# Splitting the end of the first layer's two MLPs into halves of 256 tokens

## The chip, the cores and the metric

The kernel runs on one core of a Trainium2 chip. The metric is the device time of one execution in microseconds (us): the median of several executions. Its work is spread over five engines, each of which works through its own list of instructions in order: TensorE (PE: matmuls), VectorE (DVE), ScalarE (ACT), GpSimd (POOL) and SyncE (SP), which mostly starts transfers. Waits between engines are semaphores.

## What is computed

A trunk of two layers over 1,024 tokens of width 1,024. Each layer is a token mixer and a squared-ReLU MLP with 4,096 hidden columns, with a norm before and after each and a residual around each. The mixer of layer 1 is a diagonal state-space model (S5), that of layer 2 an attention in which an indexer picks the keys.

```python
for i in range(DEPTH):                       # 2 layers
    pre = rms_norm(h, norm_g[i, 0])
    mix = s5_mixer(pre, ...) if i % 2 == 0 else dsa_mixer(pre, ...)
    h = h + rms_norm(mix, norm_g[i, 1])
    ff = sq_relu_mlp(rms_norm(h, norm_g[i, 2]), mlp_w1[i], mlp_w2[i])
    h = h + rms_norm(ff, norm_g[i, 3])

def sq_relu_mlp(h, w1, w2):
    a = jax.nn.relu(h @ w1)
    return (a * a) @ w2
```

## The kernel before

**Layout.** Tokens are worked in two halves of 512 (half 0 and half 1). An activation is held feature-major: four blocks `[128, 2, 512]`, so that 1,024 features are 4 blocks by 2 by 128 partitions, and the 512 tokens run along the row. Every fp32 operand of a large matmul is split into a rounded part `hi` and a rest `lo`, and each product is three matmuls (`mm3`, L157 to L159). Of a weight unit (`unit`) ScalarE writes `hi` (L140), and `lo` is written by VectorE for the unit's first part and by GpSimd for its second (both L141).

**An MLP** (`mlp`) makes hidden pairs (w1) and, a chunk of them later, adds their products with w2: eight chunks c, in each four blocks d by two rows j, of 12 matmuls into one PSUM tile `m`. VectorE adds each tile to the block `acc` in SBUF (L334). The path `finish` (L310 to L320) was there already: chunk 7 loads its four w2 units first and then runs twice over them, tokens 0 to 255 and then 256 to 511, with matmuls of 256 columns and an add of 256 columns (L319), and calls `finish` after each. Before the change only the very last MLP of the program uses it.

**The end of an MLP.** `post_norm` squares the outputs on ScalarE, sums the blocks on VectorE (`squares`, L191), sums over partitions with a matmul by a column of ones (L194), takes the reciprocal root (`rsqrt`, L165 to L169), spreads it over the partitions with transposes (L236), copies that to `rb` (ScalarE, L238), scales (VectorE, L250) and adds the residual (L260: blocks 0 and 2 on VectorE, 1 and 3 on GpSimd), which is loaded into tiles `ld` from `hd`. Then `pre_norm` makes the next inputs: `hi` on ScalarE (L206), `lo` on VectorE (L207), squares, their sums (L191) and the sum over partitions (L194), and from it r (L212 to L216). `att_r` multiplies rope's table by r (L1144 on VectorE, L1151 on ScalarE) and transposes it (L1153 on TensorE); the index and query projections of layer 2 follow.

**The order on each engine.** A scheduler lays the instructions out from a simulated timeline of its own; code under `high_priority` is put forward. Beside each MLP runs other work ("side"), a step after so many of the MLP's units, and where the side work or an end waits, the matmuls of the following MLP stand between as filler. So the end of half 0's MLP in layer 1 is laid among the first w1 matmuls of half 1's MLP; the end of half 1's among the attention outputs (`att_in`) of half 0 and the next MLP's w1 matmuls. The body of `run` sets the sequence:

```python
acc = self.mlp(0, xn[1][0], first(), PER_A, WAIT_A)
xo = finished(self.att_in(0, "x"))
x1, r = self.pre_norm(residual(1, acc, 3, hd[0], hd[1], xn[1][1]), 4, square=False)
self.att_r(1, r)
```

Below, "the first end" is that of half 0's MLP of layer 1, "the second end" that of half 1's.

## Time and profile before

| | |
|---|---|
| time, median of 3 runs | 2282.32 us (2281.85 to 2283.55) |
| the profiled execution | 2287.54 us, its span 2285.6 us |
| mean granted TensorE clock | 0.971 of full speed |
| TensorE busy with matmuls | 2166.6 us, 95% |
| VectorE, ScalarE, GpSimd busy | 63%, 47%, 31% |

Everything below is read from one profiled execution, whose own time is 1.94 us over its span (from the first instruction to the last). It is 5.2 us over the median of the runs. A wait stands in brackets behind the instruction that ended it, with the engine and line that released it. "PEclk" is the clock granted to TensorE, as a share of full speed.

### The profile page before, as it was taken

How to read it: one execution, taken by the hardware profiler on the slowest of the kernel's cores; microseconds unless marked ns; L12 is line 12 of the kernel's file. 1: busy time of each engine (PE TensorE's matmuls, PEld its weight loads, DVE VectorE, ACT ScalarE, POOL GpSimd, SP SyncE). 2: the span in 40 equal slices, each digit the busy share in tenths (PEclk: the TensorE clock that was granted, in tenths of full speed). 3: DMA queues.
4: the chain of work that ended last, by engine and by line, in shares of the span. 5: the costliest groups of instructions: out<-in, count | busy, mean ns of one | idle time of the engine just before them, and what ended most of it. 6: DMA issues, size and time to landing. Idle time of an engine off the chain costs nothing.

```text
span 2285.6 us, 29529 instructions
## 1 busy us (share of the span) xinstructions
PE 2166.6 (95%) x10376; PEld 1785.5 (78%) x10376; DVE 1436.7 (63%) x2775; ACT 1083.0 (47%) x2027; POOL 701.8 (31%) x588
## 2 busy tenths in 40 slices
PE   6999999999989999999988988999999899999996
PEld 3577778888878888888877766888788687888886
DVE  9566953333656598555677898989767467332335
ACT  4434643333353475555363455677457354423332
POOL 2004542222336522221346533221210035222223
PEclk9999999999999999999989999999999999999998
DMA  7002533333337653445346543433332444433231
GB/s 276 27 30 83 181 123 94 100 95 100 111 114 204 165 134 107 119 101 167 132 159 157 154 119 81 110 86 92 88 84 60 134 131 164 138 95 99 93 105 51
DMA packets 115893, 266.81 MB, mean 117 GB/s; under 512 B 14241, under 2 KB 49569, under 8 KB 115745
## 3 DMA queue, kind: packets, MB, share of 16 engines
q1 hardware_dynamic: 101984, 240.80, 33.9%
q0 software_dynamic: 12672, 23.07, 5.3%
q8 instruction: 82, 1.34, 0.3%
q10 hardware_dynamic: 1088, 1.05, 0.1%
q14 instruction: 67, 0.54, 0.1%
HBM read 229.02 MB, written 34.67 MB: 115 GB/s over the span
## 4 chain that ended last, share of the span: by engine, by line
PE 73%; DVE 15%; ACT 6%; issue 4%; DMA 1%; POOL 1%; SPq 0%; ACTq 0%; DVEq 0%; POOLq 0%
PE m L158 18%; PE m L157 18%; PE m L159 18%; PE p L1036 2%; PE p L1056 2%; PE p L157 2%; PE p L159 2%; PE p L158 2%; DVE wh L141 2%; PE p L1064 1%; DVE b L250 1%; PE p L1065 1%; ACT junk L974 1%; DVE b L207 1%; PE m L611 1%
## 5 line engine op out<-in xcount | busy, mean ns | idle before, releaser
L157 PE MATMUL m<-b,wh 128*128 128x512 f32 (+1 forms) x2208 | 860.5, 392 | 26.1 <-DVE acc L334 9.7
L158 PE MATMUL m<-b,wh 128*128 128x512 f32 (+1 forms) x2208 | 858.0, 391 | 4.6 <-DVE b L207 4.0
L159 PE MATMUL m<-b,wh 128*128 128x512 f32 (+1 forms) x2208 | 856.3, 390 | 4.3 <-DVE wh L141 4.3
L141 POOL TENSOR_TENSOR wh<-wr,wh 128x512 fp32r<-128x512 f32 (+1 forms) x346 | 448.7, 1302 | 1281.6 <-ACT wh L140 1261.6
L140 ACT ACTIVATE wh<-wr 128x512 fp32r<-128x512 f32 (+1 forms) x692 | 400.0, 592 | 503.2 <-PE m L159 413.9
L157 PEld LDWEIGHTS m<-b,wh 128*128 128x128 f32 x2208 | 419.4, 190 | 115.8 <-DVE acc L334 10.8
L159 PEld LDWEIGHTS m<-b,wh 128*128 128x128 f32 x2208 | 418.9, 190 | 88.8 <-DVE wh L141 5.1
L158 PEld LDWEIGHTS m<-b,wh 128*128 128x128 f32 x2208 | 419.2, 190 | 87.3 <-DVE b L207 4.8
L141 DVE TENSOR_TENSOR wh<-wr,wh 128x512 fp32r<-128x512 f32 (+1 forms) x346 | 273.4, 797 | 296.8 <-ACT wh L140 283.2
L334 DVE TENSOR_TENSOR acc<-acc,m 128x512 f32<-128x512 f32 x216 | 147.1, 682 | 155.5 <-PE m L159 153.5
L299 ACT ACTIVATE b<-m 128x512 f32<-128x512 f32 x128 | 76.2, 595 | 179.0 <-PE m L159 175.8
L148 DVE CAST b<-b 128x1024 fp32r<-128x1024 f32 x68 | 59.9, 881 | 135.5 <-ACT b L301 126.4
L159 PE MATMUL p<-b,wh 128*128 128x512 f32 (+1 forms) x304 | 116.1, 391 | 8.4 <-DVE wh L141 8.4
L157 PE MATMUL p<-b,wh 128*128 128x512 f32 (+1 forms) x304 | 115.8, 398 | 5.7 <-ACT b L721 3.4
L158 PE MATMUL p<-b,wh 128*128 128x512 f32 (+1 forms) x304 | 117.3, 391 | 0.0
L1043 ACT ACTIVATE s<-s,ring 128x128 f32<-128x128 f32 (+7 forms) x128 | 98.6, 772 | 36.6 <-DVE ring L1040 35.4
L1061 DVE TENSOR_TENSOR pt<-p,pt 128x512 fp32r<-128x512 f32 (+1 forms) x160 | 99.1, 630 | 22.3 <-ACT pt L1060 22.0
L1060 ACT ACTIVATE pt<-p 128x512 fp32r<-128x512 f32 (+1 forms) x160 | 83.5, 551 | 60.4 <-PE p L1056 59.5
L974 ACT ACTIVATE junk<-b,ring 128x512 bf16<-128x512 f32 (+2 forms) x90 | 80.7, 896 | 64.8 <-DVE ring L970 59.4
L1036 PE MATMUL p<-kt,q 128*128 128x512 f32 (+2 forms) x384 | 100.2, 365 | 1.5 <-DVE pt L1061 1.2
L1056 PE MATMUL p<-con,s 128*128 128x128 f32 x576 | 93.1, 273 | 0.0
L1040 DVE CUSTOM_DVE_ANT_0 s<-p,nb 128x512 f32<-128x512 f32 (+3 forms) x128 | 72.6, 582 | 25.4 <-PE p L1036 25.2
(304 smaller groups left out, 2738.0 us busy)
## 6 DMA issues: line engine op xcount, KB each, us to landing
wr<-in_w_dram SPq DMA_DIRECT2D x256, 512.0 KB, 3.6
wr<-in_wa_dram SPq DMA_DIRECT2D x32, 512.0 KB, 3.7
q<-qd POOLq DMA_DIRECT2D x64, 256.0 KB, 5.4
ld<-hd SPq DMA_DIRECT2D x24, 512.0 KB, 6.2
hd<-b SPq DMA_DIRECT2D x16, 512.0 KB, 4.4
qd<-b SPq DMA_DIRECT2D x128, 64.0 KB, 2.1
wr<-in_wao_dram SPq DMA_DIRECT2D x16, 512.0 KB, 3.6
q<-qi POOLq DMA_DIRECT2D x24, 256.0 KB, 4.8
```

Of the source, the lines that this page charges most:

```text
L140: nc.scalar.activation(ph, pr, AF.Copy)
L141: (nc.gpsimd if h else nc.vector).tensor_sub(pl, pr, ph.bitcast(F32))
L157: mm(ps, w[0], x[0], start=start, stop=False)
L158: mm(ps, w[0], x[1], start=False, stop=False)
L159: return mm(ps, w[1], x[0], start=False, stop=stop)
L334: nc.vector.tensor_add(acc[d][:, j], acc[d][:, j], ps)
L974: nc.scalar.activation(junk[:, 1, :W[j]], keys[j].bitcast(F32), AF.Sign, bias=neg[:, j:j + 1], accum_out=cnt[:, j:j + 1])
L1036: nc.tensor.matmul(ps[:, :m], qt[:, v, 2 * hp + k, :], self.K[c][g // 2][:, g % 2, :m], start=v == 0, stop=v == 1)
L1043: nc.scalar.activation(s, s, AF.Exp, bias=least, scale=-1.0, accum_out=self.sums[:, h:h + 1])
L1056: nc.tensor.transpose(pt[:, kk, k, :], P[k][:, (k0 + kk) * 128:(k0 + kk + 1) * 128], self.ident)
L1060: nc.scalar.activation(ph[:, :nk], pt[:, :nk], AF.Copy)
L1061: nc.vector.tensor_sub(pl[:, :nk], pt[:, :nk], ph.bitcast(F32)[:, :nk])
```

## The change

Both MLPs of layer 1 get the path `finish`. The function handed over (`take`) is called after each half of 256 tokens and does for it what followed the whole MLP before: `post_norm` with the residual loaded and stored in half-width pieces (256 KB, eight loads and eight stores per end in place of four and four of 512 KB), and `pre_norm` into half of the tiles `x` and `r`, which are allocated ahead. Side work that is left over is issued before chunk 7 instead of after it. In the second MLP the split of half 0's attention outputs (`att_in(0, "x")`) is issued before the norm of the first 256 tokens, so within the MLP, where it stood after the MLP before.

```diff
--- before.py
+++ after.py
@@ -194,13 +194,13 @@
             nc.tensor.matmul(ps[:, j:j + 1], acc[:, j * 128:(j + 1) * 128], self.ones, start=True, stop=True)
         return ps[:, :n // 128]
 
-    def pre_norm(self, h, gi, tag="b", square=True):
+    def pre_norm(self, h, gi, tag="b", square=True, into=None):
 
 
         nc = self.nc
         out = []
         for j, b in enumerate(h):
-            hi, lo = [self.blk([128, 2, 512], F32R, tag=tag) for _ in range(2)]
+            hi, lo = into[0][j] if into else [self.blk([128, 2, 512], F32R, tag=tag) for _ in range(2)]
             for q in range(2):
                 g = self.gain[:, gi, 2 * j + q:2 * j + q + 1]
                 nc.scalar.activation(hi[:, q], b[:, q], AF.Copy, scale=g)
@@ -208,12 +208,13 @@
                                                op0=ALU.mult, op1=ALU.subtract)
             out.append((hi, lo))
         s = self.squares(h, nc.gpsimd.tensor_add if square else nc.vector.tensor_add)
-        r = self.small([128, 4], F32, "kept")
+        r = into[1] if into else self.small([128, 4], F32, "kept")
         nc.vector.tensor_scalar(r, s, 1.0 / 1024, EPS, op0=ALU.mult, op1=ALU.add)
         if square:
             nc.vector.scalar_tensor_tensor(r, r, 1024 * EPS, r, op0=ALU.mult, op1=ALU.mult)
         else:
-            nc.vector.tensor_copy(r, self.rsqrt(r, 4)[:, :4])
+            n = r.shape[-1]
+            nc.vector.tensor_copy(r, self.rsqrt(r, n)[:, :n])
         return out, r
 
     def post_norm(self, f, gi, h, e=None, reorder=False, last=None, aside=False):
@@ -307,6 +308,8 @@
             while len(hid) < min(2 * c + 3 + (c >= 6), 16):
                 pair(len(hid))
             if finish and c == 7:
+                for _ in side or ():
+                    pass
                 ws = [self.unit(w2[L, c, d], last=True) for d in range(4)]
                 for th in range(2):
                     n = slice(256 * th, 256 * th + 256)
@@ -1227,9 +1230,32 @@
             self.store_h(dst[hf], h)
             return h
 
+        def halves(hf, first=lambda: None):
+
+
+            x = [tuple(self.blk([128, 2, 512], F32R) for _ in range(2)) for _ in range(4)]
+            r = self.small([128, 4], F32, "kept")
+
+            def take(n, f):
+                if not n.start:
+                    first()
+                m = slice(n.start // 128, n.stop // 128)
+
+                def load(j):
+                    t = self.blk([128, 2, 512], name="ld", tag="ld")[:, :, :256]
+                    self.nc.sync.dma_start(t, hd[0][hf][j][:, :, n])
+                    return t
+
+                h = self.post_norm(f, 3, [lambda j=j: load(j) for j in range(4)], xn[hf][1][:, m])
+                for j in range(4):
+                    self.nc.sync.dma_start(hd[1][hf][j][:, :, n], h[j])
+                self.pre_norm(h, 4, square=False, into=([[t[:, :, n] for t in b] for b in x], r[:, m]))
+
+            return take, x, r
+
         self.nc.sync.dma_start(self.rope, a["rope"])
-        acc = self.mlp(0, xn[0][0])
-        x1, r = self.pre_norm(residual(0, acc, 3, hd[0], hd[1], xn[0][1]), 4, square=False)
+        take, x1, r = halves(0)
+        self.mlp(0, xn[0][0], finish=take)
         self.att_r(0, r)
         self.att_start()
 
@@ -1238,9 +1264,11 @@
             yield from self.projections(0, x1)
             yield from self.attention_a()
 
-        acc = self.mlp(0, xn[1][0], first(), PER_A, WAIT_A)
-        xo = finished(self.att_in(0, "x"))
-        x1, r = self.pre_norm(residual(1, acc, 3, hd[0], hd[1], xn[1][1]), 4, square=False)
+        side = first()
+        xo = []
+        take, xb, r = halves(1, lambda: xo.extend(finished(self.att_in(0, "x"))))
+        self.mlp(0, xn[1][0], side, PER_A, WAIT_A, finish=take)
+        x1 = xb
         self.att_r(1, r)
         for _ in self.att_out(xo, "hid"):
             pass
```

The rows that follow are orders of instructions, without times. A row is a line of the program, its operation, the tile written, the tiles read and the shape. In the changed program lines from L197 on stand one to three higher: L251 is the L250 of before, L261 the L260, L322 the L319, L1039 the L1036. Matmuls count three rows to a `mm3`.

**TensorE, first end.** Before, the pre-norm's sum over partitions is one group of four for all 512 tokens, `c_531`, 136 matmuls of 512 columns after the transposes of the post-norm:

```order
L159 MATMUL m_570_4563<-b554_4425,wh567_1_4545 128x512
L157 MATMUL m_570_4563<-b554_4425,wh567_1_4545 128x512
L194 MATMUL c_531_4241<-con_72,b527_4225 128x1 x4
L158 MATMUL m_570_4563<-b555_4426,wh567_1_4545 128x512
L159 MATMUL m_570_4563<-b554_4425,wh567_1_4545 128x512
L157 MATMUL m_573_4586<-b547_4351,wh571_0_4579 128x512
```

In the changed program the pre-norm of the first 256 tokens (`c_532`) and the post-norm of the second 256 (`c_548`) stand six matmuls apart, and this is reached 68 wide matmuls after the MLP's last:

```order
L158 MATMUL m_591_4574<-b285_1774,wh590_1_4571 128x512
L194 MATMUL c_532_4237<-con_72,b528_4221 128x1 x2
L159 MATMUL m_591_4574<-b284_1773,wh590_1_4571 128x512
L157 MATMUL m_591_4574<-b284_1773,wh590_1_4571 128x512
L158 MATMUL m_591_4574<-b285_1774,wh590_1_4571 128x512
L159 MATMUL m_591_4574<-b284_1773,wh590_1_4571 128x512
L157 MATMUL m_593_4608<-b278_1755,wh592_0_4602 128x512
L158 MATMUL m_593_4608<-b279_1756,wh592_0_4602 128x512
L194 MATMUL c_548_4375<-con_72,b544_4359 128x1 x2
L159 MATMUL m_593_4608<-b278_1755,wh592_0_4602 128x512
L157 MATMUL m_593_4608<-b278_1755,wh592_0_4602 128x512
```

and the pre-norm of the second 256 tokens, `c_563`, comes 88 wide matmuls after the transposes of its post-norm:

```order
L157 MATMUL m_610_4773<-b594_4635,wh607_1_4755 128x512
L158 MATMUL m_610_4773<-b595_4636,wh607_1_4755 128x512
L194 MATMUL c_563_4445<-con_72,b559_4429 128x1 x2
L159 MATMUL m_610_4773<-b594_4635,wh607_1_4755 128x512
L157 MATMUL m_610_4773<-b594_4635,wh607_1_4755 128x512
```

So what was one group after a chain of whole blocks is two after chains of half blocks, the first of which lies under the MLP's last matmuls. From `c_531`, and now from `c_563`, it is some 26 to 28 wide matmuls to the first transposes of `att_r`.

**VectorE, first end.** Before, from the scale (L250) on; `acc` is the MLP's output, `ld` the residual, `wh` a weight unit:

```order
L250 SCALAR_TENSOR_TENSOR acc314_2033<-acc314_2033,con_72,rb_514_4175 128x512 x2
L250 SCALAR_TENSOR_TENSOR acc318_2070<-acc318_2070,con_72,rb_514_4175 128x512 x2
L250 SCALAR_TENSOR_TENSOR acc322_2107<-acc322_2107,con_72,rb_514_4175 128x512 x2
L250 SCALAR_TENSOR_TENSOR acc326_2144<-acc326_2144,con_72,rb_514_4175 128x512 x2
L151 TENSOR_TENSOR b548_4352<-b542_4281,b547_4351 128x1024
L141 TENSOR_TENSOR wh559_0_4466<-wr559_4464,wh559_0_4466 128x512
L260 TENSOR_TENSOR acc314_2033<-acc314_2033,ld515_4177 128x1024
L260 TENSOR_TENSOR acc322_2107<-acc322_2107,ld517_4187 128x1024
L141 TENSOR_TENSOR wh563_0_4505<-wr563_4503,wh563_0_4505 128x512
L207 SCALAR_TENSOR_TENSOR b520_4202<-acc314_2033,con_72,b519_4201 128x512 x2
```

In the changed program the same steps for the second 256 tokens:

```order
L251 SCALAR_TENSOR_TENSOR acc323_2041<-acc323_2041,con_72,rb_554_4387 128x256 x2
L251 SCALAR_TENSOR_TENSOR acc327_2078<-acc327_2078,con_72,rb_554_4387 128x256 x2
L251 SCALAR_TENSOR_TENSOR acc331_2115<-acc331_2115,con_72,rb_554_4387 128x256 x2
L251 SCALAR_TENSOR_TENSOR acc335_2152<-acc335_2152,con_72,rb_554_4387 128x256 x2
L151 TENSOR_TENSOR b595_4636<-b589_4565,b594_4635 128x1024
L141 TENSOR_TENSOR wh607_0_4752<-wr607_4750,wh607_0_4752 128x512
L261 TENSOR_TENSOR acc323_2041<-acc323_2041,ld555_4389 128x2x256
L261 TENSOR_TENSOR acc331_2115<-acc331_2115,ld557_4399 128x2x256
L207 SCALAR_TENSOR_TENSOR b295_1806<-acc327_2078,con_72,b294_1805 128x256 x2
L141 TENSOR_TENSOR wh611_0_4789<-wr611_4787,wh611_0_4789 128x512
```

Each step has half the width in as many instructions, and about as many rows of weight units lie between. The first 256 tokens' L251, L261 and L207 now stand ahead of these, among the adds L322 of the MLP itself.

**TensorE, the last block of attention in layer 2.** Here `p` tiles are attention (L1036 scores, L1056 transposes, L1064 and L1065 products with the values, L1082), `m` tiles the MLP that runs beside it. Before, behind the seventh L1082:

```order
L1082 MATMUL p1_2593_14511<-con_72,ring_73 16x128
L1036 MATMUL p1_2597_14518<-kt611_5038,q2567_14398 128x512 x2
L1065 MATMUL p1_2582_14460<-pt2584_14466,v665_5751 128x256
L1064 MATMUL p1_2582_14460<-pt2584_14466,v665_5751 128x256
L1065 MATMUL p1_2582_14460<-pt2584_14466,v665_5751 128x256
L1036 MATMUL p1_2599_14522<-kt1538_10065,q2567_14398 128x512 x2
L1064 MATMUL p1_2582_14460<-pt2586_14478,v666_5756 128x256
L1036 MATMUL p1_2601_14527<-kt611_5038,q2567_14398 128x512 x2
L1065 MATMUL p1_2582_14460<-pt2586_14478,v666_5756 128x256
```

In the changed program (L1085 is the L1082 of before), a few rows behind the seventh:

```order
L1059 MATMUL p1_2647_14877<-con_72,s2606_14698 128x128
L159 MATMUL m_2818_15608<-b2642_14860,wh2817_0_15602 128x512
L157 MATMUL m_2818_15608<-b2642_14860,wh2817_0_15602 128x512
L158 MATMUL m_2818_15608<-b2643_14861,wh2817_0_15602 128x512
L159 MATMUL m_2818_15608<-b2642_14860,wh2817_0_15602 128x512
L1039 MATMUL p1_2661_14926<-kt1600_10469,q2629_14802 128x512 x2
L1067 MATMUL p1_2644_14864<-pt2648_14882,v706_5966 128x256
L1039 MATMUL p1_2663_14931<-kt651_5248,q2629_14802 128x512 x2
L1039 MATMUL p1_2665_14935<-kt1600_10469,q2629_14802 128x512 x2
```

Before, no matmul of an MLP is left for this place; now 64 wide matmuls that stood ahead of the seventh L1082 lie behind it. The shift begins in the middle of the attention of half 1 (none up to the first scores, 21 at the 145th L1036, 74 at the 193rd, 84 at most) and is gone at the 353rd.

## Rows read from the trace of the kernel before

**Rows 1.** The page: engines' busy time, and the chain that ended last.
```profile
PE 2166.6 (95%) x10376; PEld 1785.5 (78%) x10376; DVE 1436.7 (63%) x2775; ACT 1083.0 (47%) x2027; POOL 701.8 (31%) x588
...
PE 73%; DVE 15%; ACT 6%; issue 4%; DMA 1%; POOL 1%; SPq 0%; ACTq 0%; DVEq 0%; POOLq 0%
```

**Rows 2.** Timeline of TensorE, first end: start us, us, instruction, idle before it.
```profile
603.67 0.95 PE L194 MATMUL c<-con,b 128*128 128x1 f32 x8
604.48 0.49 PE L159 MATMUL m<-b,wh 128*128 128x512 f32 x1
...
610.52 0.60 PE L236 MATMUL c<-con,ring 128*128 128x128 f32 x4
...
641.36 0.39 PE L157 MATMUL m<-b,wh 128*128 128x512 f32 x1
645.58 1.84 PE L194 MATMUL c<-con,b 128*128 128x1 f32 x8 [3.83 <-DVE b L191]
...
655.47 0.60 PE L1153 MATMUL p<-con,b 128*128 128x128 f32 x4
657.99 0.33 PE L1153 MATMUL p<-con,b 128*128 128x128 f32 x1 [1.92 <-ACT b L1151]
```

**Rows 3.** Windows of 5 us, first end: busy time of each engine, PEclk, DMA.
```profile
645.00:650.00 5.00, 4.42 (x15) 3.87 (x16) 4.52 (x12) 1.41 (x4) 0.93 (x2) 0.51 0.39 108
```

**Rows 4.** Groups of VectorE by line, 612 to 646 us: busy us, mean ns.
```profile
L250 DVE SCALAR_TENSOR_TENSOR acc<-acc,con,rb 128x512 f32<-128x512 f32 x8 | 8.6, 1135 | 0.0
L207 DVE SCALAR_TENSOR_TENSOR b<-acc,con,b 128x512 fp32r<-128x512 f32 x8 | 6.7, 870 | 0.0
L191 DVE TENSOR_TENSOR b<-b,b 128x512 f32<-128x512 f32 x6 | 6.1, 1013 | 0.4
L260 DVE TENSOR_TENSOR acc<-acc,ld 128x1024 f32<-128x1024 f32 x2 | 5.6, 2862 | 0.0
L141 DVE TENSOR_TENSOR wh<-wr,wh 128x512 fp32r<-128x512 f32 x5 | 3.4, 679 | 0.0
L151 DVE TENSOR_TENSOR b<-b,b 128x1024 fp32r<-128x1024 f32 x2 | 2.4, 1209 | 0.0
```

**Rows 5.** Timeline of VectorE, first end.
```profile
612.09 8.56 DVE L250 SCALAR_TENSOR_TENSOR acc<-acc,con,rb 128x512 f32<-128x512 f32 x8
...
644.75 0.69 DVE L191 TENSOR_TENSOR b<-b,b 128x512 f32<-128x512 f32 x1
```

**Rows 6.** Timeline of TensorE, second end.
```profile
1153.80 0.39 PE L159 MATMUL m<-b,wh 128*128 128x512 f32 x1
1156.23 1.08 PE L194 MATMUL c<-con,b 128*128 128x1 f32 x8 [2.05 <-DVE b L191]
...
1165.22 0.66 PE L1153 MATMUL p<-con,b 128*128 128x128 f32 x4 [1.46 <-ACT b L1151]
1167.32 1.12 PE L1153 MATMUL p<-con,b 128*128 128x128 f32 x4 [1.44 <-ACT b L1151]
```

**Rows 7.** Timeline of TensorE, last MLP: its change to 256 columns.
```profile
2239.98 0.39 PE L158 MATMUL m<-b,wh 128*128 128x512 f32 x1
...
2243.15 0.28 PE L157 MATMUL m<-b,wh 128*128 128x256 f32 x1
...
2254.18 0.28 PE L159 MATMUL m<-b,wh 128*128 128x256 f32 x1
```

**Rows 8.** Groups of VectorE by line, end of the last MLP (256 columns).
```profile
L191 DVE TENSOR_TENSOR b<-b,b 128x256 f32<-128x256 f32 x9 | 5.1, 568 | 2.6 <-ACT b L184 1.4 <-ACT b L187 1.1
L250 DVE SCALAR_TENSOR_TENSOR acc<-acc,con,rb 128x256 f32<-128x256 f32 x8 | 4.7, 660 | 1.3 <-ACT rb L238 1.3
```

**Rows 9.** Windows of 25 us, attention of half 1 in layer 2.
```profile
1550.00:1575.00 25.00, 25.00 (x147) 21.69 (x146) 23.72 (x72) 19.22 (x36) 3.79 (x4) 1.00 0.35 91
1750.00:1775.00 25.00, 23.39 (x160) 20.12 (x158) 21.21 (x53) 20.02 (x37) 0.00 (x0) 1.00 0.18 53
```

**Rows 10.** What TensorE waited for, 1725 to 1800 us: total, times, longest.
```profile
PE p L1064 <- ACT pt L1060: 2.4, 6, 0.7
```

## The prediction, written before the changed kernel was timed

> **What bounds the kernel now.** I read the page first: TensorE is busy 95% of the span, and 73% of the chain that ended last is TensorE, 15% VectorE [rows 1]. So only two things move the time: more or slower matmul work, and the few places where TensorE stands still. I then listed TensorE's waits around the two ends that the diff touches, and read each as a timeline.
>
> At the first end TensorE meets one long wait. It starts a matmul at 641.36 and then nothing until the pre-norm's sum over partitions (L194) at 645.58, after 3.83 us of waiting for VectorE's last sum L191 [rows 2]. The wait costs more than itself: in the 5 us behind it the granted clock is 0.51, near the lower of its two levels (1.2 of 2.4 GHz), with TensorE busy for 4.42 of the 5 [rows 3]. The first transposes of `att_r` (L1153) come at 655.47. Between lie that matmul and 26 more of 512 columns, and the L194. At full clock 14 wide matmuls take 3.17 us, 0.2264 each from start to start (2239.98 to 2243.15) [rows 7], and the L194 group 0.81 us where it did not wait (603.67 to 604.48) [rows 2]. So 14.11 us hold 27 x 0.2264 + 0.81 = 6.92 us of work: 7.2 us are lost. A second wait, 1.92 us for ScalarE's L1151, follows at 657.99 [rows 2].
>
> At the second end the same L194 waits 2.05 us, and L1153 is reached at 1165.22, 11.42 us after the matmul at 1153.80 [rows 6]. Less the 1.46 us that L1153 itself waits, and less 22 x 0.2264 + 0.81 = 5.79 us of work, 4.2 us are lost. Then 1.44 us more go at the second L1153.
>
> Why is the sum late? VectorE at the first end starts the scale L250 at 612.09 and ends its last L191 at 644.75 + 0.69 = 645.44 [rows 5]: 33.4 us in which the norm's own instructions are 8.6 + 6.7 + 6.1 + 5.6 = 27.0 us, and nearly all the rest weight units and splits for TensorE (L141, L151) [rows 4], with next to no idle time. The whole chain stands behind the last of the MLP's outputs; TensorE's filler ran out 3.83 us early.
>
> **What the change takes away.** The chain is cut in two, and the first half starts under the MLP's last matmuls. 96 narrow matmuls at 0.120 us (92 of them from 2243.15 to 2254.18, 11.03 us) [rows 7] make 11.5 us per half, so the first 256 tokens are complete 11.5 us before the second. In the order of the changed program the last L194 of the first end stands 88 wide matmuls behind its transposes: 19.9 us, and 0.4 for the transposes. VectorE needs for the second 256 tokens half of the 27.0 us, 13.5, and as the narrow forms are not quite half (0.660 against 1.135 us for L250, 0.568 against 1.013 for L191 [rows 4, 8]) some 0.1 us more for each of 8 L250 and 0.06 for each of 8 L191, so about 14.8; between them stand one L151 and three L141, 1.2 + 2.0 [rows 4]. From the transposes (610.52 [rows 2]) to the scale (612.09 [rows 5]) it took 1.6. That is 14.8 + 3.2 + 1.6 = 19.6 us against 20.3: the sum is there 0.7 us before TensorE asks. At the second end 79 wide matmuls give 17.9 + 0.4 = 18.3, and VectorE has 14.8, two L141 (1.4), one wide L191 (1.0) and the 1.6: 18.8, so 0.5 late. For the first half at the first end (`c_532`) TensorE gives from its transposes on 25 narrow and 68 wide matmuls, 3.0 + 15.4 = 18.4 us. VectorE needs the 14.8, the 1.6, one L141 (0.7) and six narrow adds and sums of the other half that stand between (0.57 each, 3.4): 20.5, or 2.1 us late. These are durations of instructions that run beside GpSimd's; the 2.86 us of an L260 [rows 4] may well be less when GpSimd's own L260 is shorter, and then `c_532` is in time as well.
>
> So the two big waits, 7.2 + 4.2 = **11.4 us**, go, but what takes their place lies within two microseconds of a wait, on both sides. A wait once taken at `c_532` moves TensorE back and spares the later ones, so they don't add up. I take a **remainder of 2.0 us** for both ends together (bounds 0 and 6: nothing late; or 1.5 us at each end with as much again for a clock that falls, as after the 3.83 us wait, where it cost about as much as the wait). The waits at L1153 (1.92; 1.46 and 1.44) stay: from the last sum to `att_r` the steps on VectorE and ScalarE are the same, only at the second end fewer matmuls cover them (14 for 21, 1.6 us) while VectorE has fewer sums left in between. I set that to nothing.
>
> **What it adds.** Per end 192 matmuls of 256 columns replace 96 of 512: 192 x 0.1199 = 23.0 us for 96 x 0.2264 = 21.7, 1.3 more, **2.6 us** for both. They are at full clock in a stretch without a wait, so it is all on the path. The Trainium skill (TensorE: Matmul & The Clock Gate, section "Wait — 56ns, not 53.3ns?") has matmuls follow each other at columns / 2.4 GHz plus a fixed 2.5 ns or so; by that it would be 109.2 and 215.8 ns, an estimate of 0.25 us per end. The rows here are slower for both widths and the narrow one more so, so the rows decide; by the page the forecast would be 2 us lower.
>
> Two L194 groups of two and two transposes of two for one of four: the same passes, with breaks in the stream. Between nothing and half a slot of 0.81 each [rows 2]; I take **0.6 us** for both ends.
>
> Twice as many loads and stores of the residual, each half as large, hold the same bytes. GpSimd's L260 may wait for its fourth tile, as its buffer comes free only when the one before it is added; that is covered by VectorE's own L250, L260 and L207, and would come out as a late `c_563`, in the remainder's bounds. The four w2 units of chunk 7 at once cost nothing: where the last MLP goes over to narrow matmuls in the same way (2243.15), no gap stands before the first of them [rows 7]. Their split needs ScalarE and VectorE while the fill of w1 pairs still feeds TensorE. Splitting the attention outputs inside the second MLP moves VectorE work ahead of the chain and out of it; at nothing, since VectorE stands idle for part of the stretch before the scale; without that cover the first half's scale starts later by what of it VectorE still has to do, and `c_1454`, the sum of the first half there, is the next to be late.
>
> **The second layer's order moves too.** Up to 84 wide matmuls of the MLP, 19 us, go from the middle of half 1's attention to its last block. Where they leave, TensorE is busy 25.00 of 25 us and VectorE 23.7; where they go, TensorE is busy 23.4 and VectorE 21.2 [rows 9], and TensorE waits 2.4 us in six pieces for ScalarE [rows 10]. The work is the same; it gains those waits if it fills them (-2.4), and loses if VectorE sets the pace where it leaves. Bounds -4 and +8; I take nothing, between rows that point either way.
>
> **The sum.** -11.4 + 2.0 + 2.6 + 0.6 = -6.2 us. Against the profiled execution's 2287.5 that is 2281.3; the runs' median lies 5.2 us under it, with the same work in both, so 2282.3 - 6.2 = **2276.1 us**.
>
> **Rivals.**
> *The wait comes back in halves.* VectorE has some 86 more rows, and the margins are about 1 us. If each chain is 15% slower than reckoned, 3 us, then `c_532` or `c_563` waits 2 to 3 us at either end, the clock falls behind it, and half of the 11.4 us is gone again: -5.7 + 3.2 = -2.5, 2279.8 us. For it speaks that VectorE had no idle time in the chain; against it, that it had idle time ahead of it, which the first half now takes.
> *The filler is missed in the attention (slower).* Between the 145th and the 305th L1036 VectorE is busy 95% [rows 9]. If it, not TensorE, sets the pace there, TensorE idles in the place of the moved matmuls, and those 19 us are added at the end, less what VectorE saves by the adds that go with them. It decides from 6.2 us on; at a little over half of the 19, 11 us, the time is 2287. Against it: 25.00 of 25 us busy means that TensorE was the later one.
> *The last block gains.* The moved matmuls fill the waits of [rows 10]: 2276.1 - 2.4 = 2273.7.
> *The clock does not fall as before* in the stretch of L1153, since no long wait stands ahead of it; this gives another 1 to 2 us, with the forecast otherwise as it is.
>
> **How the numbers follow.** The forecast, with or without the two small gains, has 0.6; the wait in halves 0.22; the filler missed 0.18. A measurement here tells about 0.2%, 4.6 us, from no change. The forecast lies 6.2 under, so a little of its spread falls within 4.6 and the rest is faster; the wait in halves counts mostly as no change; the filler case is split. Faster 0.56, same 0.26, slower 0.18. The likeliest case alone is 2270 to 2279; with the other cases' bounds the range is 2267 to 2287.
>
> **What would show it.** Right: TensorE's list of waits has no L194 wait over 1.5 us at either end and the granted clock stays at 1.00 up to the first L1153; 12 matmuls of an `m` tile in chunk 7 take 1.44 us; L1153's waits of 1.4 to 1.9 us are still there; chunk 7 starts at the same time as before. Wrong: an L194 or L236 of 2 us or more with a clock near 0.5 behind it; a new wait at chunk 7's first matmul for `wh`; more waits for VectorE between 1540 and 1700, or a stretch from the second end to the end of the attention that is longer than before.

## The result, and the profile after

The changed kernel takes 2270.39 us (median of 6 runs, 2267.89 to 2276.93) against 2283.03 us (6 runs of the kernel before, 2281.85 to 2288.71). The ratio is 0.9943, with a 95% interval of 0.9931 to 0.9955: 13.0 us faster (10.3 to 15.8), where 6.2 were forecast. The profiled execution is the fastest of the six, 2267.89 us with a span of 2266.1; that span lies 19.5 us under the one of the profiled execution of before, which was 4.5 us over its median. So the two traces differ by more than the change is worth, and the places have to be told apart from chance.

The page of the changed kernel: busy time by engine, and the chain that ended last, beside [rows 1].

```profile
PE 2153.7 (95%) x10568; PEld 1784.9 (79%) x10568; DVE 1445.8 (64%) x2877; ACT 1086.9 (48%) x2069; POOL 704.3 (31%) x592
...
PE 78%; DVE 12%; issue 3%; ACT 3%; POOL 2%; DMA 1%; SPq 0%; DVEq 0%; ACTq 0%; POOLq 0%
```

TensorE's share of the chain rises from 73% to 78%, VectorE's falls from 15% to 12%. TensorE's busy time falls too, by 12.9 us, although its matmuls have the same columns in all: the mean granted clock of this execution is 0.978, that of the one before was 0.971.

**First end.** Timeline of TensorE in the changed kernel (start us, us, instruction, idle before it in brackets), where [rows 2] had the wait of 3.83 us:

```profile
592.17 0.38 PE L237 MATMUL c<-con,ring 128*128 128x128 f32 x2
...
610.93 0.50 PE L194 MATMUL c<-con,b 128*128 128x1 f32 x4
...
612.78 0.50 PE L194 MATMUL c<-con,b 128*128 128x1 f32 x4
...
619.12 0.38 PE L237 MATMUL c<-con,ring 128*128 128x128 f32 x2
...
639.31 0.50 PE L194 MATMUL c<-con,b 128*128 128x1 f32 x4
...
648.85 0.33 PE L1156 MATMUL p<-con,b 128*128 128x128 f32 x1 [2.09 <-ACT b L1154]
```

The sums of the first half (610.93), the second post-norm (612.78) and the second pre-norm (639.31) are reached without a wait. The wait before the second group of rope transposes stays, 2.09 against 1.92 us. Windows of 5 us there (busy time of PE, PEld, DVE, ACT, POOL, then the granted clock, DMA):

```profile
635.00:640.00 5.00, 5.00 (x26) 4.21 (x25) 4.86 (x8) 4.98 (x10) 2.85 (x2) 1.00 0.25 78
640.00:645.00 5.00, 5.00 (x23) 4.12 (x22) 4.52 (x12) 1.34 (x5) 1.45 (x2) 1.00 0.44 134
645.00:650.00 5.00, 2.91 (x15) 2.21 (x14) 0.90 (x3) 3.80 (x9) 1.40 (x2) 0.95 0.44 127
650.00:655.00 5.00, 5.00 (x18) 3.93 (x17) 0.69 (x1) 0.63 (x1) 0.00 (x0) 0.71 0.22 86
```

The clock is 1.00 where the last sum stands, and falls only behind that wait: to 0.95 and 0.71, where it was 0.51 in [rows 3]. Whether it falls there differs from trace to trace, and nothing here tells why. The six experiments below that have this first end show the same wait of 2.1 us, and in five of them the clock stays at 1.00 behind it (in split_only it falls to 0.69). So in first_only:

```profile
650.00:655.00 5.00, 2.94 (x17) 2.22 (x16) 0.76 (x2) 3.15 (x8) 1.40 (x2) 1.00 0.53 148
```

VectorE for the second 256 tokens, from the scale to the last sum, beside [rows 5]:

```profile
621.39 4.28 DVE L251 SCALAR_TENSOR_TENSOR acc<-acc,con,rb 128x256 f32<-128x256 f32 x8
...
628.43 2.37 DVE L261 TENSOR_TENSOR acc<-acc,ld 128x512 f32<-128x512 f32 x2
...
638.35 0.41 DVE L191 TENSOR_TENSOR b<-b,b 128x256 f32<-128x256 f32 x1
```

From the transposes (619.12) to the end of the last sum (638.35 + 0.41) it is 19.6 us, the figure of the prediction; TensorE asks at 639.31, some 0.5 us later.

**Second end.** TensorE, beside [rows 6]:

```profile
1097.01 0.61 PE L194 MATMUL c<-con,b 128*128 128x1 f32 x4 [0.72 <-DVE b L191]
...
1146.62 0.50 PE L194 MATMUL c<-con,b 128*128 128x1 f32 x4
...
1154.53 1.07 PE L1156 MATMUL p<-con,b 128*128 128x128 f32 x4 [4.07 <-ACT b L1154]
1156.81 1.12 PE L1156 MATMUL p<-con,b 128*128 128x128 f32 x4 [1.21 <-ACT b L1154]
...
1202.74 0.80 PE L159 MATMUL p<-b,wh 128*128 128x512 f32 x1 [8.11 <-DVE wh L141]
```

The wait of 2.05 us at the L194 is gone as well. But the rope transposes now wait 4.07 and 1.21 us (1.46 and 1.44 before), the first post-norm's sum waits 0.72, and later a projection waits 8.11 us for a weight unit, where the kernel before waited twice (2.39 and 3.87 us). What stands ahead of the rope on VectorE, in the changed kernel:

```profile
1145.13 2.72 DVE L191 TENSOR_TENSOR b<-b,b 128x256 f32<-128x256 f32 x3
1147.77 1.83 DVE L141 TENSOR_TENSOR wh<-wr,wh 128x256 fp32r<-128x256 f32 x2
1149.53 2.20 DVE L191 TENSOR_TENSOR b<-b,b 128x512 f32<-128x512 f32 x3
1151.65 0.15 DVE L212 TENSOR_SCALAR con<-c 128x2 f32<-128x2 f32 x1
```

and in the kernel before:

```profile
1161.24 1.40 DVE L191 TENSOR_TENSOR b<-b,b 128x512 f32<-128x512 f32 x2
1162.56 0.15 DVE L212 TENSOR_SCALAR con<-c 128x4 f32<-128x4 f32 x1
```

TensorE's sum of the second half began at 1146.62 and took 0.50. VectorE comes to it (L212) at 1151.65: two pieces of weight units and three wide sums (1149.53) of the attention outputs' norm stand before it in VectorE's order. That is 4.53 us after the sum's end, and the rope's transposes follow 7.41 us after it (1154.53). Before, the sum ended at 1157.31 (1156.23 + 1.08, [rows 6]), VectorE came to L212 5.25 us after it, and the transposes followed after 7.91 us (1165.22). So in both kernels the chain over VectorE, and then ScalarE's L1151 (now L1154), sets this stretch, and its length hardly changed.

**Where the time went, stage by stage.** In all these programs the matmuls that read a weight unit into a tile `m`, nearly all of them the MLPs', come in one order, so one can be found again by its number. Ahead of each number in the table TensorE has done the same other matmuls in all thirteen kernels; this matters, as their orders differ in between: ahead of number 3300, for one, the full change has done 8 matmuls of the indexer's scores (L906) more than before, 1.4 us of work that would pass for a loss at the second end. The table gives the start of the matmul with that number (counted from 0, a narrow one as half), less its start in the profile of before; a change from one column to the next is what the stage between them gave (minus) or cost. The last rows are the experiments below.

| number of the `m` matmul | 1440 | 1860 | 2940 | 3311 | 3600 | 4560 |
|---|---|---|---|---|---|---|
| stage that ends there | S5, MLP | first end | attention A | second end | indexer of half 1 | attention of half 1 |
| before, start us | 575.34 | 769.47 | 1083.92 | 1239.56 | 1393.94 | 1806.36 |
| full change | -3.52 | -9.96 | -11.66 | -11.55 | -16.11 | -19.34 |
| first_only | 0.85 | -7.22 | -8.95 | -9.75 | -9.75 | -9.33 |
| second_only | 6.80 | 5.93 | 4.43 | 4.77 | 6.03 | 6.71 |
| late_split | 0.09 | -7.97 | -9.60 | 10.09 | 10.39 | 10.69 |
| narrow_only | 0.04 | 1.15 | 3.22 | 6.67 | 8.13 | 8.45 |
| nudge_before | 6.53 | 5.63 | 3.93 | 4.05 | -0.06 | -0.20 |
| nudge_control | 3.90 | 3.11 | 1.37 | 0.29 | 0.38 | 0.76 |
| nudge_first | 0.18 | -7.86 | -9.43 | -11.95 | -16.25 | -17.03 |
| nudge_second | 3.94 | 3.38 | 1.69 | 5.92 | 1.66 | 0.48 |
| pool_sums | 0.12 | -7.87 | -9.53 | -9.33 | -16.02 | -17.49 |
| split_only | -1.10 | -7.58 | -9.01 | -9.44 | -9.39 | -10.89 |
| first_pool | 0.06 | -7.97 | -9.57 | -8.62 | -12.91 | -13.54 |

For the full change: 3.5 us before any changed instruction (chance: the first column runs from -3.5 to 6.8), 6.4 at the first end, 1.7 in attention A (chance too: all kernels but narrow_only show 1.4 to 1.7), a loss of 0.1 at the second end, then 4.6 in the indexer's stretch of half 1 and 3.2 in its attention, where the diff changes nothing. With the first end in halves the column 1860 gives 6.4 and 6.5 us in the two kernels whose clock falls behind the rope's wait, and 8.0 to 8.1 in the five where it doesn't. Of each some 0.8 is chance, as kernels with the old first end and whole chunks gain 0.6 to 0.9 there.

### The profile page after: what moved, and what is told of

It reads as the page before. It is cut to its first block, busy times and chain, and to the rows that moved or that the text cites. A ratio compares the mean times of both kernels' runs of the same rounds, so it can differ in the third digit from the quotient of the medians.

```text
span 2266.1 us, 30101 instructions
## 1 busy us (share of the span) xinstructions
PE 2153.7 (95%) x10568; PEld 1784.9 (79%) x10568; DVE 1445.8 (64%) x2877; ACT 1086.9 (48%) x2069; POOL 704.3 (31%) x592
## 4 chain that ended last, share of the span: by engine, by line
PE 78%; DVE 12%; issue 3%; ACT 3%; POOL 2%; DMA 1%; SPq 0%; DVEq 0%; ACTq 0%; POOLq 0%
PE m L157 19%; PE m L158 19%; PE m L159 19%; PE p L1039 2%; PE p L1059 2%; PE p L157 2%; PE p L159 2%; PE p L158 2%; PE p L1068 1%; PE p L1067 1%; PE m L614 1%; DVE wh L141 1%; DVE b L207 1%; POOL b L191 1%; PE p L906 1%
## 5 line engine op out<-in xcount | busy, mean ns | idle before, releaser
L157 PE MATMUL m<-b,wh 128*128 128x512 f32 (+1 forms) x2272 | 869.6, 385 | 18.7 <-DVE acc L337 8.0
L158 PE MATMUL m<-b,wh 128*128 128x512 f32 (+1 forms) x2272 | 866.3, 383 | 4.6 <-DVE b L207 4.0
L159 PE MATMUL m<-b,wh 128*128 128x512 f32 (+1 forms) x2272 | 865.8, 383 | 3.3 <-DVE wh L141 3.3
L141 POOL TENSOR_TENSOR wh<-wr,wh 128x512 fp32r<-128x512 f32 (+1 forms) x346 | 448.1, 1300 | 1242.5 <-ACT wh L140 1146.3
L157 PEld LDWEIGHTS m<-b,wh 128*128 128x128 f32 x2272 | 430.5, 190 | 103.6 <-DVE acc L337 11.6
L158 PEld LDWEIGHTS m<-b,wh 128*128 128x128 f32 x2272 | 430.3, 189 | 84.7 <-DVE b L207 4.8
L159 PEld LDWEIGHTS m<-b,wh 128*128 128x128 f32 x2272 | 430.0, 189 | 85.0 <-DVE wh L141 4.1
L141 DVE TENSOR_TENSOR wh<-wr,wh 128x512 fp32r<-128x512 f32 (+1 forms) x346 | 272.9, 796 | 298.5 <-ACT wh L140 288.3
L337 DVE TENSOR_TENSOR acc<-acc,m 128x512 f32<-128x512 f32 x200 | 135.9, 682 | 134.7 <-PE m L159 133.4
L159 PE MATMUL p<-b,wh 128*128 128x512 f32 (+1 forms) x304 | 114.4, 386 | 9.7 <-DVE wh L141 9.7
L157 PE MATMUL p<-b,wh 128*128 128x512 f32 (+1 forms) x304 | 114.2, 393 | 3.4 <-ACT b L724 3.4
L158 PE MATMUL p<-b,wh 128*128 128x512 f32 (+1 forms) x304 | 115.9, 386 | 0.0
L1064 DVE TENSOR_TENSOR pt<-p,pt 128x512 fp32r<-128x512 f32 (+1 forms) x160 | 99.0, 630 | 24.6 <-ACT pt L1063 24.4
L1039 PE MATMUL p<-kt,q 128*128 128x512 f32 (+2 forms) x384 | 98.5, 363 | 0.0
L151 DVE TENSOR_TENSOR b<-b,b 128x1024 fp32r<-128x1024 f32 x68 | 91.5, 1345 | 1.2
```

Of the source, the lines that this page charges most:

```text
L141: (nc.gpsimd if h else nc.vector).tensor_sub(pl, pr, ph.bitcast(F32))
L151: (nc.gpsimd if lo_pool else nc.vector).tensor_sub(lo, x, hi.bitcast(F32))
L157: mm(ps, w[0], x[0], start=start, stop=False)
L158: mm(ps, w[0], x[1], start=False, stop=False)
L159: return mm(ps, w[1], x[0], start=False, stop=stop)
L337: nc.vector.tensor_add(acc[d][:, j], acc[d][:, j], ps)
```

## The experiments

After the result theory A was: the first end gives about 6 us, the second nothing, and the rest comes from the other order that the scheduler made in layer 2. Theory B: the two ends give it all. Four kernels that undo a part each tell them apart, as the order of layer 2 differs among them.

**first_only.** The second MLP as before.

```diff
-        side = first()
-        xo = []
-        take, xb, r = halves(1, lambda: xo.extend(finished(self.att_in(0, "x"))))
-        self.mlp(0, xn[1][0], side, PER_A, WAIT_A, finish=take)
-        x1 = xb
+        acc = self.mlp(0, xn[1][0], first(), PER_A, WAIT_A)
+        xo = finished(self.att_in(0, "x"))
+        x1, r = self.pre_norm(residual(1, acc, 3, hd[0], hd[1], xn[1][1]), 4, square=False)
```

> Only the first MLP ends in halves; the second end and the whole order of layer 2's attention are those of before. Theory A (the first end gives about 6 us, the second end nothing on balance, the rest of the 13 us comes from the other order of the MLP's matmuls beside layer 2's attention): 6 us under before, about 2277, and the waits between 1230 and 1450 and the attention as before. Theory B (the two ends give it all, the order of layer 2 nothing): also about 6 to 7 us under before.

Measured: 2277.57 us against 2285.02, ratio 0.9967 (0.9954 to 0.9980): 7.5 us. In the table 8.1 at the first end (some 0.8 of it chance), and nothing from 3311 on. As both theories had it.

**second_only.** The first MLP as before.

```diff
-        take, x1, r = halves(0)
-        self.mlp(0, xn[0][0], finish=take)
+        acc = self.mlp(0, xn[0][0])
+        x1, r = self.pre_norm(residual(0, acc, 3, hd[0], hd[1], xn[0][1]), 4, square=False)
```

> Only the second MLP ends in halves (with the split of the attention outputs inside it); layer 2 gets nearly the order of the full change. Theory A: the second end about as long as before, layer 2 shorter by 6 to 7 us: about 2276.5, and the waits of the indexer's stretch (1240 to 1450) shorter than before. Theory B: the same time, but the gain shows before the first indexer scores of half 1, and from there on the distance to before stays constant.

Measured: 2287.72 us, ratio 1.0015 (1.0003 to 1.0027): 3.4 us slower. Neither theory had that. In the table the second end costs 0.3, the indexer's stretch is 1.3 longer than before (4.77 to 6.03) and the attention 0.7, although 84 matmuls have moved to the last block of attention as in the full change. Against the kernels that keep the whole second end, which gain up to 2.5 us there, the loss at the second end is larger (see below). B falls; A is wrong in what of the order it credits. The two orders agree from the 193rd L1036 on and differ in the indexer's stretch: ahead of the 289th projection matmul of L157 stand 10 fewer wide matmuls of the MLP than before in the full change, and 24 fewer here. So the moved matmuls in the attention are worth nothing, and what remains is the order in the indexer's stretch.

**late_split.** The full change, but the attention outputs are split after the second MLP.

```diff
-        xo = []
-        take, xb, r = halves(1, lambda: xo.extend(finished(self.att_in(0, "x"))))
+        take, xb, r = halves(1)
         self.mlp(0, xn[1][0], side, PER_A, WAIT_A, finish=take)
+        xo = finished(self.att_in(0, "x"))
```

> Both MLPs end in halves, but the attention outputs are split after the second MLP, as before; with that layer 2's attention has the order of before again, and the rope transposes of half 1 come ahead of the attention output matmuls. Theory A: the first end's 6 us alone, about 2277, give or take what the other place of the rope transposes does at the second end (their waits of 4.07 and 1.21 us may go or be longer, bounds -4 and +4). Theory B: about 2270, as with the full change.

Measured: 2298.78 us, ratio 1.0067 (1.0053 to 1.0081): 15.3 us slower, far outside what either theory had. TensorE at the second end, in its own trace:

```profile
1118.35 0.98 PE L194 MATMUL c<-con,b 128*128 128x1 f32 x4 [12.04 <-DVE b L191]
...
1136.16 1.65 PE L157 MATMUL m<-b,wh 128*128 128x512 f32 x3 [12.94 <-ACT b L1111]
```

With halves, the attention outputs' matmuls fill TensorE's time under the norms, and these need the split. Behind the norms it comes too late: 12.04 us of waiting for the first half's sum and 12.94 for the split (L1111), and 19.7 us in the table. Splitting inside the MLP is not an extra of the change: without it the second half of the change loses far more than the first gains.

**narrow_only.** Both last chunks run as halves of 256 columns; norm, residual and next inputs follow once, as before.

```diff
-        take, x1, r = halves(0)
-        self.mlp(0, xn[0][0], finish=take)
+        acc = self.mlp(0, xn[0][0], finish=lambda n, f: None)
+        x1, r = self.pre_norm(residual(0, acc, 3, hd[0], hd[1], xn[0][1]), 4, square=False)
```

(and the second MLP likewise, with the split after it.)

> Both MLPs run their last chunk as two halves of 256 columns, but norm, residual and next inputs follow once for all 512 tokens, as before. The order of layer 2 is nearly that of the full change. Theory A: 2.6 us for the narrow matmuls, the waits of the two L194 as before, layer 2 shorter by 6 to 7: about 2279. Theory B: 2.6 us over before, about 2285.6.

Measured: 2294.97 us, ratio 1.0047 (1.0034 to 1.0060): 10.7 us slower. The first end's chunk costs 1.3 us (its offset goes from 0.04 to 1.34 over the chunk), as forecast, and its L194 waits 4.09 us. The second end costs 3.5, and the indexer's stretch, in nearly the order of second_only, 1.5 (6.67 to 8.13). Both theories missed, by 8 us and more. Of that 2.1 us lie in attention A, where one wait is 1.9 us here, 1.2 in the profile of before and nothing in first_only; that much is chance in part.

Theory C from these: first end 6 to 7 us, second end a loss of 1 to 2, and the full change's order of the indexer's stretch 9. Theory D: that order is worth nothing either, and the halves leave something behind that makes the stretch faster. To change the order alone, a few writes of four columns are put on VectorE behind the second MLP: they do nothing but shift the scheduler's simulated timeline. 32 of them give the kernel before the full change's order from the indexer on; 64 leave it as it was.

**nudge_before** and **nudge_control.** The kernel before with 32 and 64 writes.

```diff
         self.att_r(1, r)
+        z = self.small([128, 4], F32, "kept")
+        for _ in range(32):
+            self.nc.vector.memset(z, 0.0)
```

> The kernel before with 32 tiny writes of VectorE (4 columns each) put behind the second MLP, which do nothing but shift the scheduler's own timeline: both ends as before, and layer 2 laid out as in the full change. Theory C (of the 13 us the first end gives 6 to 7, the second end costs 1 to 2, and the order of the indexer's stretch of half 1 that the scheduler happened upon gives 9): 9 us under before less 1 to 2 for the writes, about 2277. Theory D (the order is worth nothing, the stretch is faster because of what the halves themselves leave behind): before or 1 to 2 us over it, about 2285 to 2287.

> The same with 64 writes, which leave the order of layer 2 as it was before: the price of the writes alone. Both theories: 0 to 6 us over before (64 writes at under 0.1 us each, mostly in time that VectorE has free).

Measured: nudge_before 2282.18 us, ratio 0.9983 (0.9973 to 0.9994), 3.9 us faster with no half anywhere; nudge_control 2285.69, ratio 0.9995 (0.9982 to 1.0008), no difference. In the table the indexer's stretch is 4.1 us shorter in nudge_before (4.05 to -0.06), as the time says, and 0.1 longer in the control. D falls; C has the sign and the place, and its size is too large. What TensorE waits for there, 1238 to 1455 us (line, releaser: us in total, times, longest), in nudge_before:

```profile
PE m L157 <- DVE acc L334: 4.3, 3, 2.1
PE p L159 <- DVE wh L141: 2.8, 1, 2.8
PE m L157 <- ACT b L299: 2.7, 4, 0.7
PE p L157 <- ACT wh L140: 2.7, 1, 2.7
PE p L158 <- DVE wh L141: 2.0, 1, 2.0
PE m L157 <- DVE ring L992: 1.1, 1, 1.1
PE p L903 <- DVE b L802: 1.1, 1, 1.1
PE m L157 <- ACT acc L332: 0.7, 1, 0.7
```

and in the control:

```profile
PE m L157 <- ACT b L299: 4.5, 5, 1.4
PE p L159 <- DVE wh L141: 4.1, 2, 2.8
PE p L903 <- DVE b L802: 3.1, 1, 3.1
PE m L157 <- DVE acc L334: 2.9, 2, 2.1
PE m L157 <- DVE ring L992: 2.5, 1, 2.5
PE p L157 <- ACT wh L140: 2.3, 1, 2.3
PE m L157 <- ACT acc L332: 1.6, 1, 1.6
```

It is no one wait. The scores (L903) wait 1.1 instead of 3.1 us and the MLP's filler (`m`) 8.8 instead of 11.5 in all; the projections (`p` at L157 to L159) wait more, 7.5 against 6.4. Over this window the waits sum to 17.4 and 21.0 us.

**nudge_first** and **nudge_second.** first_only with 32 of these writes, second_only with 16; both get the full change's order of the indexer's stretch.

> Only the first MLP in halves, and 32 writes with which layer 2 is laid out as in the full change. Theory C: 7.5 us from the first end and 9 from the order, less 1 to 2 for the writes, about 2270; as fast as the full change or faster, without the second MLP in halves. Theory D: as with the first MLP alone, about 2278 to 2280.

> Only the second MLP in halves, and 16 writes with which the indexer's stretch is laid out as in the full change (without them its order was a third one, and the time 2.7 us over before). Theory C: 9 us less than that, about 2279. Theory D: as without the writes, about 2288.

Measured: nudge_first 2271.74 us, ratio 0.9939 (0.9923 to 0.9954), 14.0 us: level with the full change, with half of it. nudge_second 2286.52, ratio 0.9997 (0.9984 to 1.0010). The order is thus worth 6.4 us beside first_only, 4.1 beside second_only, 2.7 to 3.9 beside the kernel before, by differences of ratios, which their intervals leave open by some 4 us each; in the table's stretch 4.1 to 4.6 in five of the six kernels that have it (6.7 in pool_sums). C's first end holds, its 9 us do not.

**pool_sums.** The full change, with the wide sums that stood before L212 moved to GpSimd.

```diff
-        xn[0] = self.pre_norm(residual(0, fA, 5, hd[1], hd[2]), 6, tag="x")
+        xn[0] = self.pre_norm(residual(0, fA, 5, hd[1], hd[2], sums=self.nc.gpsimd.tensor_add), 6, tag="x")
```

(`post_norm` passes `sums` on to `squares`.)

> The full change, and the sums of squares of half 0's attention outputs (L191, 128x512) on GpSimd instead of VectorE; TensorE's order is the same. In the full change the reciprocal root of half 1's second 256 tokens (L212) started on VectorE 4.5 us after its sum over partitions had ended, with three of these sums (2.2 us) and two pieces of a weight unit ahead of it, and the rope transposes waited 4.07 and 1.21 us. Theory E (those sums in VectorE's queue are what the second end lost): the first of these waits falls to about 2 us, 2 to 3 us under the full change, about 2268. Rival F (GpSimd is slower and the next norm's L194 takes the wait over): that L194, which did not wait, waits 2 to 5 us, and the time is 0 to 3 us over the full change, 2270 to 2273.

Measured: 2269.36 us, ratio 0.9949 (0.9934 to 0.9964): no different from the full change. E had the first step right: no wait is left at the first group of rope transposes (1.86 at the second). But time is lost just before it, by neither theory's way. TensorE:

```profile
1151.04 0.99 PE L194 MATMUL c<-con,b 128*128 128x1 f32 x4 [3.86 <-DVE b L191]
...
1161.09 0.66 PE L1156 MATMUL p<-con,b 128*128 128x128 f32 x4 [1.86 <-ACT b L1154]
```

It waits 3.86 us for VectorE's last narrow sum. VectorE and GpSimd at that place:

```profile
1141.84 1.54 DVE L191 TENSOR_TENSOR b<-b,b 128x256 f32<-128x256 f32 x1
...
1146.25 2.92 DVE L207 SCALAR_TENSOR_TENSOR b<-acc,con,b 128x256 fp32r<-128x256 f32 x2
```

```profile
1141.81 1.29 POOL L191 TENSOR_TENSOR b<-b 128x512 f32<-128x512 f32 x1 [0.69 <-ACT b L184]
...
1147.44 1.45 POOL L191 TENSOR_TENSOR b<-b,b 128x512 f32<-128x512 f32 x1
```

The same two steps of VectorE in the full change, with GpSimd idle:

```profile
1140.53 0.42 DVE L191 TENSOR_TENSOR b<-b,b 128x256 f32<-128x256 f32 x1
...
1143.40 0.87 DVE L207 SCALAR_TENSOR_TENSOR b<-acc,con,b 128x256 fp32r<-128x256 f32 x2
```

A narrow L191 on VectorE takes 1.54 us beside GpSimd's L191, where it took 0.42. Two L207 take 2.92, beside an L191 of GpSimd and the L141 of a weight unit before it, where they took 0.87. The work left VectorE's list and slowed what stayed there.

**split_only.** first_only, with the split of the attention outputs as the last of the second MLP's side work.

```diff
-        acc = self.mlp(0, xn[1][0], first(), PER_A, WAIT_A)
-        xo = finished(self.att_in(0, "x"))
+        xo = []
+
+        def then():
+            yield from first()
+            xo.extend(finished(self.att_in(0, "x")))
+
+        acc = self.mlp(0, xn[1][0], then(), PER_A, WAIT_A)
```

> The first MLP in halves, the second MLP whole, but the attention outputs split as the last of its side work, within the MLP; the order of layer 2 is that of before. Theory G (the place of the split alone costs and gains nothing where the end is whole, since its matmuls stand behind the MLP in TensorE's order in both): as with the first MLP alone, about 2277.6. Rival: VectorE and ScalarE are freed behind the second MLP, and the L194 wait of 2.05 us and its clock go: 3 to 4 us less, about 2274.

Measured: 2276.02 us, ratio 0.9968 (0.9959 to 0.9978), as first_only; the L194 still waits 2.04 us. G holds: beside a whole end the place of the split is worth nothing. This trace shows one thing more at the second end, which has its old order here:

```profile
1147.22 1.02 PE L194 MATMUL c<-con,b 128*128 128x1 f32 x8 [2.04 <-DVE b L191]
1156.23 0.66 PE L1156 MATMUL p<-con,b 128*128 128x128 f32 x4 [3.08 <-ACT b L1154]
```

The granted clock did not fall behind the L194 here (1.00 up to 1156 us, where the profile of before has 0.71 from 1155 to 1160), and yet the transposes come 7.99 us after the sum's end, no sooner than the 7.91 of before: they wait 3.08 us in place of 1.46.

**first_pool.** nudge_first, with the sums on GpSimd as in pool_sums.

> The first MLP in halves, the second whole, the order of layer 2 as in the full change (by 32 tiny writes), and the sums of half 0's attention outputs on GpSimd. Theory E: the reciprocal root of half 1 has no such sums ahead of it here either, and the L1156 waits (1.80 and more) get shorter by up to 2 us: about 2270, level with the full change. Rival F: as with the 32 writes alone, 2272, or 1 to 3 us over it.

Measured: 2273.86 us, ratio 0.9960 (0.9948 to 0.9972), 2 us over nudge_first by the medians, 4.8 by the ratios, whose intervals overlap, and 3.5 by the table's second end. The L194 there waits 3.80 us where nudge_first's waited 2.04, and the rope's transposes 0.65 and 1.75 us, against nothing and 1.80. So E falls; F is nearer in size and has not the place, as in pool_sums.

## Why the prediction was right in its direction, and where it was wrong

*The first end.* Right in mechanism and size: 7.2 less 1.3 for the narrow matmuls and 0.3 for the broken groups, 5.6, was forecast ahead of the remainder. Less the 0.8 of chance the table has 5.6 in the full change and 7.2 in first_only, whose time says 7.5 (4.6 to 10.5). The difference is the last of the prediction's rivals, the clock that doesn't fall at the rope, put there at 1 to 2 us: it came true in five of the seven traces. The step for the second 256 tokens came out to 0.1 us (19.6). The one for `c_532` did not: 20.5 us was reckoned against 18.4, and the sum was there in time (no wait at 610.93). The reckoning had halved durations that [rows 4] show beside GpSimd's work, and the text had named this as its doubt. Eight L251 took 4.28 us there, not 5.3, and two L261 0.68 each with GpSimd's own before and after them, not 1.43:

```profile
593.16 4.28 DVE L251 SCALAR_TENSOR_TENSOR acc<-acc,con,rb 128x256 f32<-128x256 f32 x8
597.37 0.68 DVE L261 TENSOR_TENSOR acc<-acc,ld 128x512 f32<-128x512 f32 x1
...
598.64 0.68 DVE L261 TENSOR_TENSOR acc<-acc,ld 128x512 f32<-128x512 f32 x1
```

So the remainder of 2.0 us is near 0 at this end, and the narrow matmuls' 1.3 us are confirmed here by narrow_only.

*The second end.* Wrong in the sum. Of the 4.2 us that were to go with the L194's wait, 2.05 are the wait, and that went. The rest was the price of the lowered clock behind it, and this could not be gained: the matmuls that it slowed stand before transposes that wait for VectorE and ScalarE, whose chain sets the 7.9 us from the sum to the rope, with the lowered clock and without it (7.99 in split_only). Before, 21 matmuls, slowed, filled 6.4 us of that stretch; now 14 at full clock fill 3.3 of 7.4, and the rest is wait. So the term "I set that to nothing", for the rope behind it, measured 2.4 us (4.07 + 1.21 against 1.46 + 1.44). VectorE's wide sums and weight units ahead of L212 are not what changed, as they stood there before too. Besides, the post-norm's sum waits 0.7 and the narrow matmuls take 1.3; what gave some of this back is not taken apart here.

In place of a gain of 1.6 the trace of the full change has a loss of 0.1, second_only one of 0.3 and nudge_second one of 4.2. That is against the profile of before; five kernels with the old second end (leaving out first_pool) lie between 2.5 us under it and 0.1 over. The times give a loss of 3.4 (0.7 to 6.2) in second_only, some of it the longer stretch of the indexer, of 3.2 between nudge_second and nudge_before, and of 0.9 between the full change and nudge_first, the last two by ratios whose intervals overlap. No run shows a gain at the second end; the size of the loss is not settled better than 0 to 4.

*The second layer's order.* Wrong in place and size. The prediction looked at the 84 matmuls that move into the last block of attention and took nothing, with bounds of -4 and +8. That part was right: kernels with the move and another order ahead of it gain nothing (6.03 to 6.71 in second_only). But the order also differs in the indexer's stretch, 1230 to 1400 us, of which the prediction says nothing, and there the other order is worth 4 to 5 us in the traces (6.7 in one) and 3 to 6 in the times, shown by nudge_before without any half. That this is all of what the attention of half 1 adds in the full change (3.2 us) is not: it is 0.1 to 1.5 in the other kernels with this order, and nothing here tells it from chance.

*The sum.* By its own terms the forecast of 6.2 was 4.6 from the first end and 1.6 from the second, each with half of the remainder, and nothing from layer 2. The runs show 7.5, a loss of 0 to 4, and 3 to 6 from an order that fell out by luck: 6.5 to 13.5, against 13.0 (10.3 to 15.8) measured. The forecast gave the second end 2 to 6 us too much, the first 3 too little, and had no word of the order. With the old order in the indexer's stretch the time would have been some 3 to 6 us longer, 2273 to 2276 by this estimate: near the 2276.1 of the forecast, but only because its errors at the two ends nearly cancel.

## What to carry to other kernels

Cutting a norm chain in halves pays where TensorE waits at its end and other matmuls stand ready to fill; the same cut gained nothing at the second end, where the next step's small instructions queue behind other work on VectorE. So read, for each step behind the cut, what stands ahead of it in its engine's list, and count a lowered clock as a loss only where the matmuls that it slows, and not another engine, decide when the next step starts. Where a scheduler orders the program, part of a measured gain may be another order elsewhere: a change that does nothing but shift the schedule, beside a control that shifts nothing, tells the two apart.

## What the runs showed of the hardware

VectorE's instructions with two inputs slow down while GpSimd runs such ones: a 128x256 sum on VectorE takes 0.42 us alone and 1.54 beside a 128x512 sum of GpSimd, and two L260 of 128x1024 took 2.86 on average [rows 4] beside GpSimd's L260 and L141, where one takes 1.21 with GpSimd idle (kernel before):

```profile
1877.97 1.21 DVE L260 TENSOR_TENSOR b<-b,ld 128x1024 f32<-128x1024 f32 x1
```

The Trainium skill (GPSIMD Engine Reference, section 1, Specifications) says that GpSimd's SBUF interfaces are shared with VectorE, with contention for VectorE's instructions with two SBUF inputs; these rows agree. In pool_sums and first_pool moving such work to GpSimd was thus no relief for a VectorE that was needed at the same moment.

TensorE's clock can differ from trace to trace at the same place: behind the same wait of 2.1 us at the first end's rope it fell in two of seven traces (to 0.71 and 0.69 in the 5 us from 650) and stayed at 1.00 in five.
